# Sorting experts by load ahead of a branch, and three smaller moves in the order of work

## The chip, the cores and the metric

One core of a Trainium2 chip runs the whole kernel. The metric is the device time in microseconds. The engines are PE (TensorE: products; its weight loads have a row of their own, PEld), DVE (VectorE), ACT (ScalarE), POOL (GpSimd) and SP (SyncE, which here only issues DMAs and handles registers). A "q" behind an engine's name is its sequencer, which waits, branches and issues.

## The reference

Two decoder layers over 512 tokens of width 1024, each a mixer and then a mixture of 16 experts, with a last RMSNorm. What the change touches is the experts' part:

```python
def hier_moe(xn, w_group, b_group, w_router, b_router, w_gate, w_up, w_down):
    glog = tf @ w_group + b_group                       # 4 groups
    gval, gsel = lax.top_k(jax.nn.softmax(glog), 1)
    elog = jnp.einsum('td,dge->tge', tf, w_router) + b_router
    ...                                                 # the chosen group's 4 experts
    top_v, top_i = lax.top_k(elog_sel, TOP_K)           # 2 of 4
    top_w = jax.nn.softmax(top_v, axis=-1) * gval
    ...
    for g in range(N_GROUPS):
        h = silu(einsum('td,edf->tef', t, w_gate[g])) * einsum('td,edf->tef', t, w_up[g])
        out = out + einsum('tef,efd->td', h * combine[:, g, :, None], w_down[g])
```

Each token goes to two experts. An expert's weights are 1024x512 (gate), 1024x512 (up) and 512x1024 (down), 2 MB each in f32.

## The kernel before

**Order of the work.** The program is traced once, in the order of the Python code; a planner then orders each engine's instructions as a list: what is traced first goes first among what its estimated times hold ready, and an idle engine takes a later instruction that is ready. `tc.issue_after(x)` puts the instructions of its block behind `x` on `x`'s engine. A `tc.If` is planned as one piece. All loads of weights are issued by SP in one queue, in order; the router's rows go to DRAM from ACT's queue; gathers and scatters of token rows go from POOL's queue.

**Router** (`router`, `chosen_of`, `ranks`). The last product of the mixer yields the tokens in four chunks of 128. For each chunk the logits come from PE (L959 for the last chunk); VectorE scales the normed rows (`rows` in the changed code, L987, two halves), which are stored to `xnd` for later gathers, and computes the logits `lg` (L989) and from them, by comparisons, which experts each token takes (L897 to L907). PE sums masks, so that each token gets its place in the list of its expert (`pos`, L904).

**Experts' start** (`moe`). `loads` reduces the counts to one number `cmax` (L1039 to L1043). `gather(0)` brings expert 0's tokens together: two chunks by a gather from DRAM (L929, L1249), two by products with one-hot matrices (L1254, which read the rows and one-hots of chunks 2 and 3). Then every engine reads `cmax` (L1410) and branches (L1411): if any list is over 128, or more than the planned number of experts are over 64, a general path computes everything (`moe_any`); the inputs here do not take it, so each engine jumps over its code. Behind the branch `by_load` ranks the experts 2 to 15 by their count (five VectorE operations, L1054 to L1058), so that heavy ones take the steps `H` (128 rows, weights split into a high and a low half for three products each) and light ones the steps `L` (64 rows, plain f32) of

`STEPS = "HHHLHHLHLHHLHHLL"`

Experts 0 and 1 keep steps 0 and 1. A product turns the ranking into ids (L1060, copied by L1062), a second one sorts the columns of `pos` (L1064, L1065). SP reads the ids into registers (L1420) and from then on loads weights by id (L1190). `listed(e)` builds an expert's one-hot from `pos` (L1012 heavy, L1017 light), sums the token numbers on PE (L1024, L1025) and writes the index (L1027); `fetch(e)` gathers the rows (L1222).

**Splits** (`wsplit`, L194). Each quarter of a heavy weight takes one ACT operation (high half), one VectorE operation (low half; for two quarters at the start, POOL) and six PE products (L197 to L199). The halves live in a ring of three, later four tiles. Raw weights live in 14 tiles of 1 MB. In `proj`, expert 0's splits are held behind the router's last one-hot, and in `gather(0)` the split of the gathered tokens behind `cmax`. In `load` the down weights of expert 1 are held behind the reads of the ids.

**Router parameters** (`router_params`, L855 to L860). Five small loads on SP into single tiles; those of layer 1 are traced in the middle of layer 1's attention (`layer1_mix`), and the planner issues them as soon as layer 0's router has read its own.

Of the kernel before, what the change touches and what calls it, by code (L numbers as in the profile page):

```python
# [37 lines left out]
    0, 128, 256, 384, 388, 389, 405, 425, 426, 427  # L38

STEPS = "HHHLHHLHLHHLHHLL"  # L40
NS = NE - 2
NHEAVY = STEPS[2:].count("H")
LIGHT = 64
# [3 lines left out]
def _constants():  # L47
# [11 lines left out]
    e_ = p % 16  # L59
    e2 = np.arange(2, 16)  # L60
    th = np.where(e2[None, :] < e_[:, None], -0.5, 0.5)
    heavy, light = iter(range(NHEAVY)), iter(range(NHEAVY, NS))
    rank = [next(heavy) if k == "H" else next(light) for k in STEPS[2:]]
    blk = np.full((128, 4, NS), -1.0)
    for i in range(64):
        if i % 16 >= 2:
            blk[i, i // 16] = rank
    own = (np.arange(16)[None, :] == e_[:, None]).astype(np.float32)
    srt = np.concatenate([blk.reshape(128, 56), own, th], 1).astype(np.float32)
    cst[:, C_EC] = e_  # L70
# [25 lines left out]
def kernel(ctx: ExitStack, tc: tile.TileContext, I, out, *_):  # L96
# [686 lines left out]
    def layer1_mix(xT, first):  # L783
# [6 lines left out]
        for hf in range(2):  # L790
# [80 lines left out]
    def router(l, wr, br, wrb):  # L871
# [9 lines left out]
        if l == 0:  # L881
            srts.append(sm.tile([128, 208], F32, bufs=1, name="srt"))
            nc.scalar.dma_start(srts[0][:, 0:86], I["srt"])
        q.srt = srts[0]
# [87 lines left out]
        def chosen_of(c, pl, s0, s1):  # L972
            xn = F[9][:, 1024 * (c % 2):1024 * (c % 2) + 1024]
            if c < 3:
                s4 = m2([128, 128], "s4")
                S.copy(s4, pl)
                pl = bank(shape=(128, 20))
                PE.matmul(pl, s4, C[:, C_SEL:C_SEL + 20], start=True, stop=True)
            rs = rstd(s0, s1, q)
            if c > 1:  # L980
                q.xn.append(xn)
            for i in range(2):
                sl = slice(512 * i, 512 * i + 512)

                a, b, o = h[:, c, sl], grow[:, sl], xn[:, sl].rearrange("q (k p) -> q p k", k=4)
                a, b = (t.rearrange("q (p k) -> q p k", k=4) for t in (a, b))
                scaled.append(V.scalar_tensor_tensor(o, a, rs, b, op0=OP.mult, op1=OP.mult))  # L987
                nc.scalar.dma_start(xnd[c * 128:(c + 1) * 128, sl], xn[:, sl])
            V.scalar_tensor_tensor(lg[:, c, :], pl, rs, br, op0=OP.mult, op1=OP.add)  # L989
            ranks(c)  # L990

        return chunk, q

    def route(q):
# [40 lines left out]
        def loads():  # L1035

            cf = sm.tile([128, 1], F32, bufs=1, name="cf")
            more, m14 = srt[:, 118:119], srt[:, 102:102 + NS]
            V.tensor_reduce(cf, pp[:, 4, :], AX.X, OP.max)  # L1039
            V.tensor_scalar(m14, pp[:, 4, 2:NE], LIGHT + 0.5, CAP / NHEAVY, op0=OP.is_gt, op1=OP.mult)  # L1040
            V.tensor_reduce(more, m14, AX.X, OP.add)
            V.tensor_tensor(cf, cf, more, op=OP.max)
            loads.last = V.tensor_copy(cmax, cf)  # L1043
            pt = bank(shape=(64, 128))
            tr(pt, pos.rearrange("p c e -> p (c e)"))
            bT = m4s[1][0:64, 0:128]
            S.copy(bT, pt)
            return cf, bT

        def by_load(bT):  # L1050

            cnt, rank, own, gt = srt[0:64, 116:117], srt[0:64, 117:118], srt[0:64, 86:102], srt[0:64, 120:134]
            P = srt[0:64, 134:190]
            V.tensor_tensor(own, srt[0:64, 56:72], pp[0:64, 4, :], op=OP.mult)  # L1054
            V.tensor_reduce(cnt, own, AX.X, OP.add)
            V.scalar_tensor_tensor(gt, pp[0:64, 4, 2:NE], cnt, srt[0:64, 72:86], op0=OP.subtract, op1=OP.is_gt)
# [8 lines left out]
            V.tensor_copy(pos[:, :, 2:NE], pm)  # L1065
            return P, ids

        def weights(P=None, fits=None):
# [29 lines left out]
            if P is not None:  # L1098
                pt = bank(shape=(64, 128))
                tr(pt, wt.rearrange("p c e -> p (c e)"))  # L1100
                wT = m4s[1][0:64, 128:256]
                S.copy(wT, pt)
                pm = bank(shape=(128, NCH, NS))
                PE.matmul(pm.rearrange("p c s -> p (c s)"), wT, P, start=True, stop=True)
                V.tensor_copy(wt[:, :, 2:NE], pm)
                V.tensor_scalar(wt, wt, fits, None, op0=OP.mult)
# [66 lines left out]
    def moe(l, rt, norm, done, then=None):  # L1173
# [6 lines left out]
        def rows_of(e, w, r0, r1):  # L1180

            rows = "(k p)" if w == "w_down" else "(p k)"
            if e < 2:
# [42 lines left out]
        def gather(e):  # L1226
# [39 lines left out]
        def proj(e, w):  # L1266
# [153 lines left out]
        got, vals = nc.values_load_multi_w_load_instructions(  # L1420
            row[0:1, :], engines=(mybir.EngineType.SP,), min_val=0, max_val=NE - 1,
            skip_runtime_bounds_check_because="sums of one-hot rows: each is one of 2 to 15, or 0")
        ids.update(zip(range(2, NE), vals))
        ids[0] = got[-1]
        listed(2, range(2))
# [88 lines left out]
```

## Time and profile before

| | us |
|---|---|
| median of 3 runs (lowest, highest) | 1144.22 (1142.65, 1145.25) |
| profiled execution | 1145.4 |
| its span, first to last instruction | 1143.6 |
| PE busy | 1050.0 (92%) |
| VectorE busy | 734.0 (64%) |
| ScalarE busy | 562.2 (49%) |

The experts of layer 0 run from about 276 to 580 us of the span, those of layer 1 from about 824 to the end. Times of rows are counted from the span's start. An idle time in square brackets or behind a bar is that of the engine just before the row's instruction, with what released it as the semaphores suggest.

### The profile page before, as it was taken

What the parts mean: (1) busy time and instruction counts of PE and PEld (TensorE: products, weight loads), DVE (VectorE), ACT (ScalarE), POOL (GpSimd) and SP (SyncE); (2) the same over time, 40 slices, a digit from 0 to 9 for tenths busy, and PEclk for the clock granted to TensorE, in tenths of its full rate; (3) what the DMA queues carried; (4) which work ended last, traced back from release to release, by engine and by line L of the source; (5) the groups of instructions that cost most, each with busy time, mean ns of one, the idle gap of its engine ahead of it and who ended that gap; (6) DMA issues with size and microseconds to landing.
All of it is one profiled execution on the core that took longest, in us unless ns stands there. A gap on an engine that the chain in (4) does not pass through costs nothing. (4 is left out here: it accounts for less than half of the span.)

```text
span 1143.6 us, 15992 instructions
## 1 busy us (share of the span) xinstructions
PE 1050.0 (92%) x5951; PEld 762.0 (67%) x5951; DVE 734.0 (64%) x1265; ACT 562.2 (49%) x852; POOL 190.1 (17%) x120
## 2 busy tenths in 40 slices
PE   5979899998799999989889999999978999999994
PEld 4766677786576765757368777877756676565641
DVE  6988952777797755756372273275679785565634
ACT  5433134524576644655353353354366675464634
POOL 3734110000312221221000000000012132211111
PEclk9999999999999999999989999999999999989998
DMA  7262323356699999999842315226349999999963
GB/s 239 74 147 104 101 78 111 107 216 240 240 381 380 380 380 383 373 374 374 309 179 75 110 37 184 74 75 234 141 170 396 354 382 392 388 385 377 367 243 147
DMA packets 84712, 277.38 MB, mean 243 GB/s; under 512 B 23714, under 2 KB 23898, under 8 KB 68368
## 3 DMA queue, kind: packets, MB, share of 16 engines
q1 hardware_dynamic: 72000, 248.31, 57.7%
q0 software_dynamic: 8016, 16.88, 5.9%
q10 hardware_dynamic: 4608, 11.06, 2.6%
q8 instruction: 51, 0.84, 0.3%
q14 instruction: 37, 0.30, 0.1%
HBM read 262.49 MB, written 24.12 MB: 251 GB/s over the span
## 5 line engine op out<-in xcount | busy, mean ns | idle before, releaser
L198 PE MATMUL acc<-R,R 128*128 128x512 f32 x936 | 381.1, 407 | 17.1 <-DVE R L194 16.3
L197 PE MATMUL acc<-R,R 128*128 128x512 f32 x860 | 350.9, 409 | 26.3 <-ACT R L194 16.5
L199 PE MATMUL acc<-R,R 128*128 128x512 f32 x860 | 342.8, 401 | 1.3 <-DVE R L194 1.3
L194 DVE TENSOR_TENSOR R<-F,R 128x1024 fp32r<-128x1024 f32 (+1 forms) x178 | 212.9, 1218 | 138.1 <-ACT R L194 133.1
L194 ACT CAST R<-F 128x1024 fp32r<-128x1024 f32 (+1 forms) x178 | 182.4, 1040 | 180.6 <-PE acc L199 107.7
L198 PEld LDWEIGHTS acc<-R,R 128*128 128x128 f32 x936 | 179.2, 191 | 67.7 <-DVE R L194 28.9
L197 PEld LDWEIGHTS acc<-R,R 128*128 128x128 f32 x860 | 164.2, 191 | 67.7 <-ACT R L194 22.5
L199 PEld LDWEIGHTS acc<-R,R 128*128 128x128 f32 x860 | 164.8, 192 | 37.7 <-DVE R L194 3.3
L1222 POOL DMA_INDIRECT F<-xnd,idx x30 | 50.9, 1698 | 238.7 <-DVE ws L1032 113.9
L1304 PE MATMUL acc<-F,R 128*64 128x512 f32 x304 | 71.2, 595 | 0.0
L194 DVE TENSOR_TENSOR R<-pb,R 128x512 fp32r<-128x512 f32 x84 | 57.3, 702 | 14.6 <-ACT R L194 14.5
L1376 POOL DMA_INDIRECT hd<-m,idx x20 | 36.6, 1829 | 147.8 <-ACT m L1375 146.0
L194 ACT CAST R<-pb 128x512 fp32r<-128x512 f32 x84 | 47.5, 586 | 27.4 <-PE pb L190 20.9
L194 DVE TENSOR_TENSOR R<-R,R 128x1024 fp32r<-128x1024 f32 x40 | 48.2, 1221 | 6.4 <-ACT R L194 6.0
L922 POOL MEMSET R<- 128x1024 f32 x2 | 1.9, 954 | 300.6 <-PE acc L199 300.6
L1304 PEld LDWEIGHTS acc<-F,R 128*64 128x64 f32 x304 | 22.0, 137 | 43.6 <-issue 43.2
L194 ACT CAST R<-R 128x1024 fp32r<-128x1024 f32 x40 | 41.4, 1050 | 13.2 <-PE acc L199 12.1
L197 PE MATMUL acc<-spare,R 128*128 128x512 f32 x116 | 45.7, 394 | 0.0
L199 PE MATMUL acc<-spare,R 128*128 128x512 f32 x116 | 45.7, 394 | 0.0
L190 PE MATMUL pb<-C,F 128*128 128x128 f32 (+1 forms) x296 | 37.5, 261 | 3.4 <-POOL F L490 3.4
L190 PE MATMUL pb<-C,m 128*128 128x128 f32 (+1 forms) x163 | 27.7, 292 | 12.7 <-DVE m L227 9.6
L1307 ACT ACTIVATE m2w<-acc 64x512 f32<-64x512 f32 x8 | 4.7, 593 | 68.5 <-PE acc L1304 68.5
(384 smaller groups left out, 1447.0 us busy)
## 6 DMA issues: line engine op xcount, KB each, us to landing
F<-in_moe_w_up_dram SPq DMA_DIRECT2D x46, 1024.0 KB, 22.4
F<-in_moe_w_down_dram SPq DMA_DIRECT2D x40, 1024.0 KB, 22.2
F<-in_moe_w_gate_dram SPq DMA_DIRECT2D x38, 1024.0 KB, 23.0
R<-in_moe_w_gate_dram SPq DMA_DIRECT2D x20, 1024.0 KB, 15.9
R<-in_moe_w_down_dram SPq DMA_DIRECT2D x12, 1024.0 KB, 24.9
h<-in_moe_w_down_dram SPq DMA_DIRECT2D x12, 1024.0 KB, 22.5
F<-in_c_w_qkv_dram SPq DMA_DIRECT2D x12, 1024.0 KB, 6.1
F<-in_ab_w_in_dram SPq DMA_DIRECT2D x10, 1024.0 KB, 5.1
```

The lines of the kernel that those rows point to most:

```text
L190: PE.transpose(dst, src, ident[:n, :n])
L194: return S.copy(hi, src), eng.tensor_tensor(lo, src, hi.bitcast(F32), op=OP.subtract)
L197: PE.matmul(ps, ah, bh, start=first, stop=False)
L198: PE.matmul(ps, ah, bl, start=False, stop=False)
L199: return PE.matmul(ps, al, bh, start=False, stop=last)
L922: G.memset(q.x0, 0.0)
L1222: rows[e] = G.indirect_dma_start(out=xg[e % 2][0:n], out_offset=None, in_=xnd[:, :], in_offset=bass.IndirectOffsetOnAxis(ap=idx[0:n, e, 0: ...
L1304: m = PE.matmul(ps[LIGHT * i:LIGHT * i + LIGHT], x_[:, 4 * kk + k, :], raw[i][:, k, :], start=kk + k == 0, stop=kk + k == 4, skip_group_ch ...
L1307: silu = S.activation(hs[0:LIGHT], ps[LIGHT:2 * LIGHT], AF.Silu)
L1376: G.indirect_dma_start(out=hd[:, :], out_offset=bass.IndirectOffsetOnAxis(ap=idx[:, e, 1:2], axis=0), in_=y[:, :], in_offset=None, bounds_ ...
```

## The change

`by_load` is traced ahead of `gather(0)` and of the branch. The split of expert 0's gathered tokens and the splits of its gate weights are held behind the last rank operation. The down weights of expert 1 are no longer held behind the ids. For the last chunk the router's ranks are traced ahead of its rows. The parameters of layer 1's router are issued behind the last weight load traced before them. The constant 2 gets a name, with the columns of the table that depend on it.

```diff
@@ constants
+FIXED = 2
 STEPS = "HHHLHHLHLHHLHHLL"
-NS = NE - 2
-NHEAVY = STEPS[2:].count("H")
+NS = NE - FIXED
+NHEAVY = STEPS[FIXED:].count("H")
...
@@ layer1_mix
             if hf == 0:
-                params = router_params(1, nc.sync)
+                with tc.issue_after(fr.load.ins):
+                    params = router_params(1, nc.sync)
@@ router, chosen_of(c, pl, s0, s1)
-            for i in range(2):
-                ...
-                scaled.append(V.scalar_tensor_tensor(o, a, rs, b, op0=OP.mult, op1=OP.mult))
-                nc.scalar.dma_start(xnd[c * 128:(c + 1) * 128, sl], xn[:, sl])
+            def rows():
+                for i in range(2):
+                    ...
+                    scaled.append(V.scalar_tensor_tensor(o, a, rs, b, op0=OP.mult, op1=OP.mult))
+                    nc.scalar.dma_start(xnd[c * 128:(c + 1) * 128, sl], xn[:, sl])
+
+            if c < 3:
+                rows()
             V.scalar_tensor_tensor(lg[:, c, :], pl, rs, br, op0=OP.mult, op1=OP.add)
             ranks(c)
+            if c == 3:
+                rows()
@@ route, by_load(bT)
-            V.tensor_scalar(P, srt[0:64, 0:56], rank, None, op0=OP.is_equal)
+            by_load.last = V.tensor_scalar(P, srt[0:64, 0:4 * NS], rank, None, op0=OP.is_equal)
@@ moe, load(e, w, r0, r1)
-            with tc.issue_after(ids[0].ins) if (e, w) == (1, "w_down") else nullcontext():
-                fr.load = nc.sync.dma_start(t, rows_of(e, w, r0, r1))
+            fr.load = nc.sync.dma_start(t, rows_of(e, w, r0, r1))
@@ moe, gather(e)
-                with after(loads.last.ins) if e == 0 else nullcontext():
+                with after(by_load.last.ins) if e == 0 else nullcontext():
                     gather.last = split_to(xh[:, 4 * i:4 * i + 4], xl[:, 4 * i:4 * i + 4], pt)
@@ moe, proj(e, w)
-                    for i in (rt.last, rt.sqrt) + (gather.last if k2 else ()) if held else ():
+                    for i in (rt.last, rt.sqrt, by_load.last) + (gather.last if k2 else ()) if held else ():
@@ moe
         cf, bT = loads()
+        perm, row = by_load(bT)
         gather(0)
         top = nc.values_load(cmax[0:1, 0:1], min_val=0, max_val=T)
         with tc.If(top > CAP):
             moe_any(l, weights(), xg[1])
         table(AF.Silu)
         ...
-        perm, row = by_load(bT)
         listed(1, range(2))
         fetch(1)
         listed(0, range(2), rt.oh)
-        got, vals = nc.values_load_multi_w_load_instructions(
+        _, vals = nc.values_load_multi_w_load_instructions(
             row[0:1, :], engines=(mybir.EngineType.SP,), min_val=0, max_val=NE - 1,
             ...
-        ids[0] = got[-1]
```

## Rows read from the trace of the kernel before

**Rows 1.** The page's second part: busy tenths of PE and of DMA in 40 slices.

```profile
PE   5979899998799999989889999999978999999994
...
DMA  7262323356699999999842315226349999999963
```

**Rows 2.** Busy us of each engine, granted clock, DMA share, GB/s by stretch.

```profile
290.00:320.00 30.00, 24.35 (x134) 18.02 (x133) 25.02 (x43) 18.84 (x24) 9.36 (x5) 0.98 0.79 293
...
350.00:560.00 210.00, 200.91 (x996) 130.98 (x994) 132.53 (x169) 116.28 (x143) 39.65 (x22) 0.99 1.00 375
590.00:690.00 100.00, 100.00 (x478) 78.94 (x476) 43.94 (x86) 39.97 (x79) 0.00 (x0) 1.00 0.25 80
```

**Rows 3.** Waits of ScalarE from 296 to 560: who for whom, us, times, longest.

```profile
ACT R L194 <- DMA F<-in_moe_w_up_dram: 0.9, 1, 0.9
```

**Rows 4.** Waits of PE from 284 to 320.

```profile
PE acc L198 <- DVE R L194: 4.9, 2, 2.6
...
PE acc L197 <- ACT R L194: 0.7, 1, 0.7
```

**Rows 5.** PE in order of time: start us, us, line, operation, idle before it.

```profile
275.21 1.91 PE L959 MATMUL pb<-wrb,m 128*128 128x20 f32 x16
...
281.45 2.05 PE L1254 MATMUL acc<-m2w,F 128*128 128x128 f32 x16
288.08 0.77 PE L197 MATMUL acc<-R,R 128*128 128x512 f32 x1 [4.58 <-DVE srt L1058]
...
292.58 0.20 PE L1060 MATMUL pb<-srt,C 64*1 64x14 f32 x2
292.71 0.42 PE L1064 MATMUL pb<-srt,m 64*128 64x56 f32 x2
...
299.89 0.50 PE L198 MATMUL acc<-R,R 128*128 128x512 f32 x1 [2.60 <-DVE R L194]
```

**Rows 6.** VectorE in order of time, the same stretch of layer 0.

```profile
276.42 2.08 DVE L987 SCALAR_TENSOR_TENSOR F<-h,rs,growt 128x512 f32<-128x512 f32 x2
278.34 0.22 DVE L989 SCALAR_TENSOR_TENSOR lg<-pb,rs,wrb 128x20 f32<-128x20 f32 x1
...
281.58 0.15 DVE L1054 TENSOR_TENSOR srt<-srt,pb 64x16 f32<-64x16 f32 x1
...
287.75 0.24 DVE L1058 TENSOR_SCALAR srt<-srt 64x56 f32<-64x56 f32 x1
...
292.81 0.16 DVE L1062 CAST srt<-pb 1x14 int32<-1x14 f32 x1 [4.28 <-PE pb L1060]
...
295.68 2.89 DVE L1017 TENSOR_TENSOR junk<-C,pos 128x512 bf16<-128x512 f32 x1
...
298.63 1.21 DVE L194 TENSOR_TENSOR R<-F,R 128x1024 fp32r<-128x1024 f32 x1
```

**Rows 7.** Sequencers at the branch (L1410, L1411): duration ns min/median/max, first and last start.

```profile
L1410 PEldq TENSOR_LOAD <-cmax x2: 312/402/491, 283.8 to 832.7; - x2
...
L1411 PEldq COMPARE_BRANCH  x2: 3328/3378/3427, 284.4 to 833.2; - x2
...
L1411 DVEq COMPARE_BRANCH  x2: 56/64/72, 285.7 to 834.4; - x2
```

**Rows 8.** SP at L1420: its wait from 281 to 330, and its reads of the ids.

```profile
SPq L1420 <- DVE el L1081: 8.0, 1, 8.0
...
L1420 SPq TENSOR_LOAD <-srt x2: 2885/2888/2891, 293.0 to 841.8; - x2
```

**Rows 9.** Layer 1: VectorE at L1062, and waits of PE from 833 to 870.

```profile
841.64 0.16 DVE L1062 CAST srt<-pb 1x14 int32<-1x14 f32 x1 [4.21 <-PE pb L1060]
...
PE acc L198 <- DVE R L194: 5.0, 2, 2.6
```

**Rows 10.** Gathers by POOL (L1222), from 297.5 to 300 and from 842 to 846.

```profile
DMA to landing us min/median/max: 9.8/9.8/9.8
...
DMA to landing us min/median/max: 4.7/4.7/4.7
```

More of the change, by code (lines that the diff above doesn't have):

```diff
@@ L38 @@
     0, 128, 256, 384, 388, 389, 405, 425, 426, 427
+FIXED = 2
 STEPS = "HHHLHHLHLHHLHHLL"
-NS = NE - 2
-NHEAVY = STEPS[2:].count("H")
+NS = NE - FIXED
+NHEAVY = STEPS[FIXED:].count("H")
+S_OWN, S_TH, S_TAB = 4 * NS, 4 * NS + 16, 5 * NS + 16
 LIGHT = 64
@@ L59, in _constants @@
     e_ = p % 16
-    e2 = np.arange(2, 16)
+    e2 = np.arange(FIXED, NE)
     th = np.where(e2[None, :] < e_[:, None], -0.5, 0.5)
     heavy, light = iter(range(NHEAVY)), iter(range(NHEAVY, NS))
-    rank = [next(heavy) if k == "H" else next(light) for k in STEPS[2:]]
+    rank = [next(heavy) if k == "H" else next(light) for k in STEPS[FIXED:]]
     blk = np.full((128, 4, NS), -1.0)
     for i in range(64):
-        if i % 16 >= 2:
+        if i % 16 >= FIXED:
             blk[i, i // 16] = rank
     own = (np.arange(16)[None, :] == e_[:, None]).astype(np.float32)
-    srt = np.concatenate([blk.reshape(128, 56), own, th], 1).astype(np.float32)
+    srt = np.concatenate([blk.reshape(128, 4 * NS), own, th], 1).astype(np.float32)
     cst[:, C_EC] = e_
@@ L882, in router @@
             srts.append(sm.tile([128, 208], F32, bufs=1, name="srt"))
-            nc.scalar.dma_start(srts[0][:, 0:86], I["srt"])
+            nc.scalar.dma_start(srts[0][:, 0:S_TAB], I["srt"])
         q.srt = srts[0]
@@ L981, in chosen_of @@
                 q.xn.append(xn)
-            for i in range(2):
-                sl = slice(512 * i, 512 * i + 512)
-                a, b, o = h[:, c, sl], grow[:, sl], xn[:, sl].rearrange("q (k p) -> q p k", k=4)
-                a, b = (t.rearrange("q (p k) -> q p k", k=4) for t in (a, b))
-                scaled.append(V.scalar_tensor_tensor(o, a, rs, b, op0=OP.mult, op1=OP.mult))
-                nc.scalar.dma_start(xnd[c * 128:(c + 1) * 128, sl], xn[:, sl])
+            def rows():
+                for i in range(2):
+                    sl = slice(512 * i, 512 * i + 512)
+                    a, b, o = h[:, c, sl], grow[:, sl], xn[:, sl].rearrange("q (k p) -> q p k", k=4)
+                    a, b = (t.rearrange("q (p k) -> q p k", k=4) for t in (a, b))
+                    scaled.append(V.scalar_tensor_tensor(o, a, rs, b, op0=OP.mult, op1=OP.mult))
+                    nc.scalar.dma_start(xnd[c * 128:(c + 1) * 128, sl], xn[:, sl])
+            if c < 3:
+                rows()
             V.scalar_tensor_tensor(lg[:, c, :], pl, rs, br, op0=OP.mult, op1=OP.add)
             ranks(c)
+            if c == 3:
+                rows()
         return chunk, q
@@ L1039, in loads @@
             V.tensor_reduce(cf, pp[:, 4, :], AX.X, OP.max)
-            V.tensor_scalar(m14, pp[:, 4, 2:NE], LIGHT + 0.5, CAP / NHEAVY, op0=OP.is_gt, op1=OP.mult)
+            V.tensor_scalar(m14, pp[:, 4, FIXED:NE], LIGHT + 0.5, CAP / NHEAVY, op0=OP.is_gt, op1=OP.mult)
             V.tensor_reduce(more, m14, AX.X, OP.add)
@@ L1050, in by_load @@
         def by_load(bT):
-            cnt, rank, own, gt = srt[0:64, 116:117], srt[0:64, 117:118], srt[0:64, 86:102], srt[0:64, 120:134]
-            P = srt[0:64, 134:190]
-            V.tensor_tensor(own, srt[0:64, 56:72], pp[0:64, 4, :], op=OP.mult)
+            cnt, rank, own, gt = srt[0:64, 116:117], srt[0:64, 117:118], srt[0:64, 86:102], srt[0:64, 120:120 + NS]
+            P = srt[0:64, 134:134 + 4 * NS]
+            V.tensor_tensor(own, srt[0:64, S_OWN:S_TH], pp[0:64, 4, :], op=OP.mult)
             V.tensor_reduce(cnt, own, AX.X, OP.add)
-            V.scalar_tensor_tensor(gt, pp[0:64, 4, 2:NE], cnt, srt[0:64, 72:86], op0=OP.subtract, op1=OP.is_gt)
+            V.scalar_tensor_tensor(gt, pp[0:64, 4, FIXED:NE], cnt, srt[0:64, S_TH:S_TAB], op0=OP.subtract, op1=OP.is_gt)
             V.tensor_reduce(rank, gt, AX.X, OP.add)
-            V.tensor_scalar(P, srt[0:64, 0:56], rank, None, op0=OP.is_equal)
+            by_load.last = V.tensor_scalar(P, srt[0:64, 0:4 * NS], rank, None, op0=OP.is_equal)
             pi = bank(shape=(1, NS))
@@ L1064, in by_load @@
             PE.matmul(pm.rearrange("p c s -> p (c s)"), bT, P, start=True, stop=True)
-            V.tensor_copy(pos[:, :, 2:NE], pm)
+            V.tensor_copy(pos[:, :, FIXED:NE], pm)
             return P, ids
@@ L1104, in weights @@
                 PE.matmul(pm.rearrange("p c s -> p (c s)"), wT, P, start=True, stop=True)
-                V.tensor_copy(wt[:, :, 2:NE], pm)
+                V.tensor_copy(wt[:, :, FIXED:NE], pm)
                 V.tensor_scalar(wt, wt, fits, None, op0=OP.mult)
@@ L1182, in rows_of @@
             rows = "(k p)" if w == "w_down" else "(p k)"
-            if e < 2:
+            if e < FIXED:
                 return wv[w][e, r0:r1, :].rearrange(f"{rows} n -> p k n", p=128)
@@ L1419, in moe @@
         listed(0, range(2), rt.oh)
-        got, vals = nc.values_load_multi_w_load_instructions(
+        _, vals = nc.values_load_multi_w_load_instructions(
             row[0:1, :], engines=(mybir.EngineType.SP,), min_val=0, max_val=NE - 1,
-            skip_runtime_bounds_check_because="sums of one-hot rows: each is one of 2 to 15, or 0")
-        ids.update(zip(range(2, NE), vals))
-        ids[0] = got[-1]
+            skip_runtime_bounds_check_because="sums of one-hot rows: each is one of FIXED to 15, or 0")
+        ids.update(zip(range(FIXED, NE), vals))
         listed(2, range(2))
```

## The prediction

> **What bounds the kernel now.** I read the slices of the page first, then the busy time by stage, then who waits for whom, and last the two engines' instructions around the branch. In the slices PE is at 9 nearly throughout, and DMA is at 9 through both expert stages [rows 1]: two resources look full there. The windows tell more. In the middle of layer 0's experts (350 to 560) PE is busy 200.91 of 210 us and DMA has a share of 1.00; in layer 1's attention (590 to 690) PE is busy 100.00 of 100 us with DMA at 0.25 [rows 2]. So outside the start of the expert stage nothing but PE's own work sets the time, as long as weights arrive. They do: in all of layer 0's expert stage ScalarE, which takes each heavy weight tile first, has only two short waits for a transfer, the longer 0.9 us [rows 3]. What is left is the start of the stage: from 290 to 320 PE is busy only 24.35 of 30 us [rows 2]. Between 284 and 320 it waits 4.9 us in two pieces for VectorE's low halves (2.6 and 2.3 us) and 0.7 us for ScalarE [rows 4], and ahead of that it stands still for 4.58 us at the branch [rows 5]. The list puts those 4.58 us down to VectorE's L1058, but the row of the branch itself says otherwise: PE's read of the count takes 0.49 us from 283.8, its COMPARE_BRANCH 3.33 to 3.43 us from 284.4, while VectorE's takes 0.07 us [rows 7]. So PE's pause is its branch, and it resumes at 288.08.
>
> Why the two later waits? VectorE finishes the fifth operation of the ranking (L1058) at 287.99, does a few small ones, and then stands 4.28 us in front of L1062, the copy of the sorted ids, because L1060, the product that makes them, sits on PE behind the branch and twelve expert products, at 292.58 [rows 5, 6]. Everything behind L1062 in VectorE's order is then late: L1017 (one-hot of expert 3) runs from 295.68 for 2.89 us, and the low half that PE needs comes only at 298.63; PE starts again at 299.89 [rows 5, 6]. Layer 1 repeats it: 4.21 us idle in front of L1062 and PE waits of 5.0 us in two [rows 9].
>
> **The change, part by part, per layer.**
>
> *Sorting ahead of the branch.* No operation is added: the same five rank operations, two products and two copies run. By the trace the ranking was already partly ahead of VectorE's branch at 285.7; what really crosses is the end of it, L1060, L1064 and the copies. (a) PE: the two products take 292.58 to 293.06, 0.48 us [rows 5]. Put behind the gather's last product (ends 283.50) they end at 283.98; PE's read of the count starts at 283.8 today [rows 7], because the count is late, so 0.3 us are hidden and about 0.2 us push the branch: +0.2. If the count comes no earlier than now and the products are held by a late rank, it is more (the slower rival). (b) Behind the branch PE has 0.48 us less: -0.48. (c) VectorE has no reason to stand in front of L1062. Into the 4.28 us go the one-hot of expert 2, the index writes, L1017, and the first operations of the weights. PE's wait of 2.6 us stems from L1017 in front of a low half; with it done early the half follows its high half directly. Bounds: 0 (L1017 stays where it is) to -2.6; I take -2.6, since 4.28 us of room hold 2.89 us of work. (d) The second pair of waits, 2.3 and 0.7 us, lies further on, where VectorE is busy 25.02 of 30 us [rows 2] and catches up only slowly. Bounds 0 to -3.0; I take a third, -1.0, because its other work there stays.
>
> *The holds.* The gather's low half and expert 0's first split now wait for the last rank operation instead of for the count and the router. Queued behind them on VectorE are the other splits of expert 0; waiting for them is PE at 288.08. VectorE needs two operations of some 1.2 us each before PE's first product (L194 in rows 6 shows one). The ranking starts at 281.58 and its last operation takes 0.24 us [rows 6]; ten such operations, the count's five among them, end by 284 as an estimate, and 2.4 us of splits by 286.4, ahead of 288.08: 0. The cover is PE's branch; were it gone, each us of ranking would cost one.
>
> *Ranks ahead of rows, last chunk.* The two row operations take 2.08 us from 276.42, and the logits came behind them at 278.34 [rows 6]. The logits need PE's products, which end at 277.12 [rows 5], so they gain about 1 us. PE is packed from 275.21 to 283.50 with the router's and the gather's products, so this shortens nothing on PE: 0. The rows must be there when the gather's last products start at 281.45 [rows 5]; if they fill VectorE's wait for the rank's sums they end some 280 to 281: 0. Their two stores on ScalarE's queue shift with them; ScalarE needs to be free for the transposed positions only after that: 0.
>
> *SP: ids earlier, expert 1's down weights earlier.* SP waits 8.0 us at L1420 and then reads the ids for 2.89 us [rows 8]. Its first load by id goes out up to 8 us earlier, and the two 1 MB loads of expert 1, no longer behind the ids, can go as soon as their tiles are free, before the branch. This moves the stream ahead and gives PE nothing, since PE does not wait for weights [rows 3]: 0; it is the cover for (c) and (d), which make PE ask earlier. One thing runs against it: POOL's gather for expert 1 meets an emptier DMA today, and one landed in 4.7 us without the stream and in 9.8 with it [rows 10]. Bounds 0 to the 5.1 us between them; I take 0, since its index is written in VectorE's gap too, some us earlier.
>
> *Router parameters of layer 1 later.* Five small loads on SP's queue move from layer 0's router into the attention, behind a weight load. There PE is 100.00 of 100 us busy and DMA is at 0.25 [rows 2]; their issue can only delay a weight load by a few us where PE never stood still: 0. The renamed constants change nothing at FIXED = 2.
>
> **Sum.** +0.2 - 0.48 - 2.6 - 1.0 = -3.9 us per layer, -7.8 for two. The bounds of (c) and (d) give -0.3 to -5.9 per layer. The profiled execution took 1145.4 us (span 1143.6 and 1.8 around it), so 1137.6 by its own time; the median of the runs is 1.2 lower, 1144.22, which gives 1136.4.
>
> **Rivals.**
>
> *The gap isn't used.* The planner that orders each engine keeps the one-hot products behind the first expert products, and L1017 in front of the same low half. Then only (a) and (b) remain, up to -0.8 per layer: 1142.6 to 1143.6. For it: the order is a list order by estimated times, and a one-hot was left unmoved in today's gap. Against: what stood in front of it there was L1062, and that is gone.
>
> *Late rows (the slower side).* The rows of the last chunk are now written behind the ranks. If VectorE takes them only after the last rank operation of the chunk (about 281.4), they end at 283.5 instead of 278.5. The gather's last products then start at 283.5 instead of 281.45, +2.05, the branch follows, and the ranking with its held splits falls as much later on VectorE, so that these splits fill the 4.28 us instead of L1017 and (c) is lost too. Net +2.05 - 0.48, about +1.6 per layer: 1147.4. It decides from the point where the rows end after 281.45, and outweighs the gain above some 283. For it: the rows have become the lower of the two in the program's order. Against: VectorE must wait for PE's sums in the middle of the ranks, and the rows are ready then.
>
> *The stream is the bound.* DMA's share of 1.00 [rows 2] suggests that the end follows the stream. Then the 8.0 us of ids [rows 8] and the 2 MB at 375 GB/s [rows 2], 5.6 us, would be gained in each layer: 27.2 us, 1117.0. Against it stand ScalarE's waits [rows 3].
>
> *A slower branch.* PE's COMPARE_BRANCH takes 3.33 to 3.43 us where VectorE's takes 0.07 [rows 7], in a stretch with DMA all but idle. If what it waits for is a transfer, the earlier weight stream can slow it as it slows a gather, 9.8 us against 4.7 us [rows 10], by 2.1 times: +3.7 per layer, which leaves 1143.8 with the gain above. It needs the 2 MB still moving at 284.4, and issued before 276 they would be done by 282. The Trainium skill, "Runtime: NRT & Kernel Launch", section "Instruction fetch mechanics", has this rule: a taken branch to a target outside the fetched window forces a DMA fetch before the engine goes on. The long row on PE alone fits it; no row yet shows such a branch under traffic.
>
> **How the numbers follow.** Chances: forecast 0.56, gap unused 0.16, late rows 0.13, stream 0.07, slower branch 0.08. What the measurement can tell from no change is 0.2%, 2.3 us: faster means below 1141.9, slower above 1146.5. The forecast and the stream lie below, with a few hundredths of the others: 0.67 faster. The unused gap and the slower branch mostly lie within: 0.20. Late rows and a little more: 0.13 slower. The forecast's own range is 1132.4 (all of (c) and (d)) to 1140.5; the range of 8 in 10 goes from 1131.5 to 1145.0, which takes in the unused gap and leaves out the stream and the late rows.
>
> **What would show it.** Right: PE's COMPARE_BRANCH still 3.3 us and PE's restart within half a microsecond of now; L1062's counterpart ahead of the branch with no 4 us gap on VectorE behind it; PE's first wait of 2.6 us gone, the second shortened; SP's first load by id 5 to 8 us earlier, with no gain from it alone; both layers alike. Wrong: the gather's last products held by the rows, a branch above 4 us, PE waiting for the gather of expert 1, or the 2.6 us at their old place.

## The result, and the profile after

The changed kernel takes 1126.85 us, the kernel before 1143.45 us on the same chip: a ratio of 0.985, with an interval of 0.983 to 0.987. It is faster by 16.6 us, more than twice the 7.8 us that I forecast and outside my range. On a second chip (e8 below) the ratio was 0.984, with 0.981 to 0.986. To read single profiles: in each profiled execution the granted clock of TensorE is 1.2 instead of 2.4 GHz in seven to fourteen stretches, 37.5 to 73.8 us in all, in part at places that differ from one execution to the next. PE's busy time changes with it: the 497 products of the late experts in the tables below are busy for 99.86 us at a mean clock of 1.00, for 102.97 at 0.98 and for 105.81 at 0.95. So I compare PE's idle time stretch by stretch (length less PE busy), and let the timed rounds speak for the sum.

The table of stretches of the kernel before, then of the changed kernel: in each the first line is the start of layer 0's experts (from the gather's last products to expert 3), the second its late experts (from expert 8 to expert 14), the third and fourth the same of layer 1. Columns: stretch, length, busy us of PE, PE's weight loads, VectorE, ScalarE, POOL, granted clock, DMA share, GB/s.

```profile
278.83:348.82 69.99, 59.12 (x339) 45.67 (x337) 61.27 (x110) 46.95 (x57) 17.20 (x10) 0.98 0.78 287
428.72:539.15 110.43, 102.97 (x497) 68.67 (x496) 71.78 (x88) 64.19 (x78) 19.81 (x12) 0.98 1.01 377
827.74:899.00 71.26, 60.43 (x339) 46.66 (x337) 60.32 (x103) 46.98 (x57) 17.19 (x10) 0.95 0.73 280
978.45:1091.77 113.32, 105.81 (x497) 70.83 (x496) 71.82 (x88) 64.23 (x78) 19.63 (x12) 0.95 1.01 381
```

```profile
276.39:344.33 67.94, 59.96 (x339) 46.77 (x337) 61.70 (x110) 47.04 (x57) 16.25 (x10) 0.95 0.76 290
424.54:526.84 102.30, 99.86 (x497) 67.80 (x497) 69.43 (x87) 62.56 (x76) 19.85 (x11) 1.00 1.01 375
818.99:886.16 67.17, 58.77 (x339) 45.88 (x337) 60.37 (x105) 47.10 (x57) 16.79 (x10) 0.97 0.75 289
966.06:1068.07 102.01, 99.55 (x497) 67.82 (x496) 69.89 (x87) 62.47 (x76) 19.78 (x11) 1.00 1.01 375
```

Length less PE busy gives the idle time. At the start it falls from 10.9 and 10.8 us to 8.0 and 8.4: 5.3 us in both layers together, the part I had forecast (with 7.8). In the late experts it falls from 7.5 and 7.5 to 2.4 and 2.5: 10.1 us, of which my forecast has nothing. The rest, from expert 14 to the next stage or the end of the kernel, idles 3.7 us more than before (12.2 to 15.9 by the gaps between PE's instructions). Together that is 11.7 of the 16.6 us. The mean granted clock of the timed runs is 0.978, that of the kernel before 0.974 to 0.975 in the experiments below; 0.3 to 0.4% of 1143 us is some 4 us as an estimate, and where this part comes from stays open. DMA's share is 1.01 in the late experts of both kernels.

The start, as it answers to [rows 4] and [rows 5]: waits of PE from 280 to 316, then its instructions there in order of time (idle time before one in brackets).

```profile
PE pb L1035 <- PEq L1422: 3.6, 1, 3.6
PE pb L1115 <- ACT m L1113: 0.9, 1, 0.9
PE pb L1036 <- issue: 0.8, 1, 0.8
PE acc L201 <- ACT R L198: 0.7, 1, 0.7
PE acc L203 <- DVE R L198: 0.7, 1, 0.7
PE acc L202 <- DVE R L198: 0.5, 1, 0.5
```

```profile
281.05 0.20 PE L1071 MATMUL pb<-srt,C 64*1 64x14 f32 x2
281.18 0.43 PE L1075 MATMUL pb<-srt,m 64*128 64x56 f32 x2
285.19 0.16 PE L1035 MATMUL pb<-tl,junk 128*128 128x2 bf16 x1 [3.59 <-PEq L1422]
...
288.46 0.16 PE L1036 MATMUL pb<-rc,m2w 128*128 128x2 bf16 x1 [0.81 <-issue]
...
296.02 0.50 PE L202 MATMUL acc<-R,R 128*128 128x512 f32 x1 [0.54 <-DVE R L198]
```

The sort's two products stand ahead of the branch; the branch holds PE for 3.59 us instead of 4.58 [rows 5]; the wait of 2.60 us is 0.54, with a new one of 0.81 ahead of it, for which the profile names no engine (the last section has what stands beside it); the second pair, 2.32 and 0.73 us in the kernel before, is 0.70 and 0.73 with 0.89 on the way. PE's branch instruction, and SP's loads of expert 1's down weights and its first load by id (columns as in [rows 7]; for SP: start us, us, operation):

```profile
L1422 PEldq COMPARE_BRANCH  x2: 3368/3488/3607, 281.7 to 824.1; - x2
```

```profile
265.51 6.09 SPq L1200 DMA_DIRECT2D R<-in_moe_w_down_dram  x2
287.47 0.37 SPq L1200 DMA_DIRECT2D F<-in_moe_w_gate_dram  x1
```

The ids' first load goes at 287.47, where the kernel before waited 8.0 us for the ids and read them from 293.0 on [rows 8], and the down weights of expert 1 go at 265.51. The queues are full then, and these loads keep them at a share of 0.89 until 276, where the kernel before has 0.38 (the same stretch of both, the kernel before first; columns as in the first table):

```profile
270.00:276.00 6.00, 5.09 (x40) 4.10 (x32) 4.82 (x16) 2.71 (x8) 2.09 (x2) 1.00 0.38 113
270.00:276.00 6.00, 5.09 (x41) 4.53 (x41) 3.86 (x17) 2.37 (x5) 0.29 (x1) 1.00 0.89 290
```

The late experts hold the surprise. In the kernel before, PE's waits there name ScalarE (5.2 us) and VectorE (1.8 us), and ScalarE's longest waits name PE; no wait of the two names a transfer. Waits of PE, then of ScalarE, from 430 to 525, and ScalarE in order of time at the first of these places:

```profile
PE acc L197 <- ACT R L194: 5.2, 6, 1.6
PE acc L198 <- DVE R L194: 1.8, 3, 0.8
```

```profile
ACT m2w L1307 <- PE acc L1304: 22.4, 2, 12.1
ACT m L1382 <- PE acc L1326: 6.2, 2, 3.1
```

```profile
435.88 0.59 ACT L1307 ACTIVATE m2w<-acc 64x512 f32<-64x512 f32 x1 [12.10 <-PE acc L1304]
436.50 0.58 ACT L194 CAST R<-pb 128x512 fp32r<-128x512 f32 x1
436.98 1.05 ACT L194 CAST R<-F 128x1024 fp32r<-128x1024 f32 x1
```

ScalarE stands 12.10 us in front of a light expert's silu (L1307), which needs PE's products, while the heavy expert's down weights stand behind it in its list; PE then waits for their split. The weights were late as well: the second of the two loads that bring them is issued at 410.4 and takes 26.0 us, so it lands at 436.4, behind the start of the silu.

```profile
DMA to landing us min/median/max: 26.0/26.0/26.0
```

In the changed kernel the same place has the other order: the splits first, waiting for their transfer, the silu behind them. Columns as above.

```profile
425.03 1.04 ACT L198 CAST R<-F 128x1024 fp32r<-128x1024 f32 x1 [1.65 <-DMA F<-in_moe_w_down_dram]
425.98 1.04 ACT L198 CAST spare<-F 128x1024 fp32r<-128x1024 f32 x1
431.70 0.59 ACT L1317 ACTIVATE m2w<-acc 64x512 f32<-64x512 f32 x1 [4.68 <-PE acc L1314]
```

```profile
ACT R L198 <- DMA F<-in_moe_w_down_dram: 12.2, 4, 7.6
```

### The profile page after: what moved, and what is told of

It reads as the page before. It is cut to its first block, busy times and chain, and to the rows that moved or that the text cites. A ratio compares the mean times of both kernels' runs of the same rounds, so it can differ in the third digit from the quotient of the medians.

```text
span 1123.5 us, 16007 instructions
## 1 busy us (share of the span) xinstructions
PE 1044.2 (93%) x5951; PEld 761.6 (68%) x5951; DVE 730.7 (65%) x1265; ACT 564.2 (50%) x852; POOL 191.1 (17%) x120
## 5 line engine op out<-in xcount | busy, mean ns | idle before, releaser
L194 PEld LDWEIGHTS pb<-C,m 128*128 128x128 f32 (+1 forms) x163 | 20.4, 152 | 27.0 <-DVE m L231 10.3
```

The lines of the kernel that those rows point to most:

```text
L194: PE.transpose(dst, src, ident[:n, :n])
```

## Experiments

All ratios are to the kernel before, timed on the same chip in turn. START is my forecast (only the start of the stage counts), STREAM or LANDING says that weights which land earlier are the gain, ORDER that it is the engines' lists, which the planner writes anew for every edit.

**One part at a time, and the order of ScalarE.** e1 lists the light expert's scatter scale behind the next heavy expert's splits; e2 puts the changed kernel's splits behind that scale; e3 and e4 are the two large parts of the change alone.

```
e1, before:  with after(wsplit.hi.ins):
                 S.activation(y, ps, AF.Copy, scale=...)       # L1382
e2, changed: late() ahead of proj(e, "w_up") where a heavy expert follows a light one;
             for e = 9, 12 its first split stands in  with after(light_scatter.last.ins)
e3, before:  load() without  tc.issue_after(ids[0].ins)  for (1, "w_down")
e4, before:  by_load(bT) ahead of gather(0) and the branch, with the holds on by_load.last
```

> The kernel before, with one edit: the scale of a light expert's scatter (L1382) is listed on ScalarE behind the four high parts of the next expert's up weights, where that expert is heavy, two places per layer. PE's list and SP's list are unchanged. Theory ORDER (the gain of the late experts is the order of ScalarE's list): the two waits of 1.55 and 0.76 us at 458, 513, 1008 and 1065 us go, 9.2 us, and the low clock behind them, 6.8 us, less what the end of the stage gives back because the last light expert's weights land only 3.2 us ahead of their use: 1130 to 1138. Theory STREAM (the gain is weights that land earlier): the loads by id are issued as late as before, no gain, 1142 to 1145. Theory START (only the start of the expert stage counts, as I forecast): 1142 to 1145.

> The changed kernel, with the first high part of the up weights of experts 9 and 12 listed on ScalarE behind the light expert's scatter scale, as the kernel before has it. SP's list is that of the changed kernel. ORDER: gives back 5 to 14 us, 1132 to 1140, with PE's two waits back at those two places of each layer. STREAM: the weights land as early as in the changed kernel, 1125 to 1128. START: 1125 to 1128.

> The kernel before, with the one edit that expert 1's down weights are no longer held behind the ids. START: nothing waits for these weights, 1142 to 1145. STREAM: most of the gain, 1127 to 1132. ORDER: its ScalarE list has the scatter scale of expert 8 behind the four high parts, but that of expert 11 ahead of them as before; so the waits at 458 and 1008 go with their low clock (2.3+1.7 and 2.3+3.4) and those at 513 and 1065 stay: 1133 to 1138.

> The kernel before, with the sort and its holds ahead of the branch; expert 1's down weights stay behind the ids, the rows stay ahead of the ranks, the router parameters early. START: the start of the expert stage alone, 2.0 us in layer 0 and 4.1 in layer 1 by the shift of PE's work in the changed kernel, so 1136 to 1138. STREAM: the ids come 8 us earlier in each layer, 1127 to 1131. ORDER: the start's 6 us, and of the late waits those behind expert 8 in part (its scale stands behind two of the four high parts): 1130 to 1135.

Measured: e1 0.996 (0.994 to 0.998), e2 0.986 (0.983 to 0.989), e3 0.994 (0.992 to 0.996), e4 0.988 (0.985 to 0.990). START falls with e3: these loads cost nothing by my reckoning, and freeing them alone gives 7 us. STREAM as I had put it falls too: e3 has half of what it asked for. ORDER does not do well by e1: the waits at 458 us and its like don't go, they change their name.

```profile
PE acc L198 <- DVE R L194: 3.9, 4, 1.7
PE acc L197 <- ACT R L194: 2.2, 4, 0.6
```

VectorE's list holds the low parts now as ScalarE's had held the high ones. e2 brings back waits of 1.55 and 0.76 us at all four places, though SP's list is that of the changed kernel, so those waits are the list's; but its late idle time is 4.8 us per layer, the changed kernel's own waits (0.55 and 1.24 us) having gone, and in time it loses 1 to 2 us by the ratios, where ORDER asked for 5 to 14; its four runs spread so far (1127.75 to 1136.04 us) that 5 is not ruled out. The late idle time of e3 (4.6 and 5.2 us) and e4 (3.9 and 4.8) lies half way between the two kernels: each alone loses the first group of waits in a layer (438 and 458 us in the kernel before) and keeps the second. In both a short wait of PE names a transfer of gate weights now (0.7 and 1.3 us in e3, 0.9 in one layer of e4). Their gains add up to 21 us, the change has 17.

**Orders fixed by hand, the small edits, a repeat.**

```
e5 = e1 and, where a heavy expert follows a light one:
        pu = proj(e, "w_up")
        with after(wsplit.hi.ins):
            gather(e + 1)
e6 = the same in the changed kernel
e7 = before with  if c == 3: rows()  behind ranks(c), and
     with tc.issue_after(fr.load.ins): params = router_params(1, nc.sync)
```

> The kernel before, with the order fixed by hand at the places where a heavy expert follows a light one (up of experts 4, 7, 9 and 12): its up projection is traced ahead of the next gather, and the gather's rows and the light expert's scatter scale are listed on ScalarE behind the four high parts. SP's list, and so the weight stream, is that of the kernel before. ORDER: the waits of 1.55 and 0.76 us at 458, 513, 1008 and 1065 us go on both engines' lists now, 9.2 us, with a part of the low clock behind them (0 to 6.8 us), less up to 2 us per layer at the end of the stage: 1131 to 1138. STREAM: no load is issued earlier for it, 1142 to 1146. START: 1142 to 1146.

> The changed kernel with the same hand-fixed order. ORDER: its own late waits are 0.55 and 1.24 us per layer (490, 502, 1031, 1043 us), 3.6 us at most to win, but its last light expert's weights land with 0.0 us to spare, so most of it comes back as waits for transfers: 1124 to 1128, not told from the changed kernel. If it wins all of 3.6 us the end of the stage isn't bound by the stream. STREAM: no change, 1125 to 1128.

> The kernel before with the two small edits alone: the router's last ranks ahead of its rows, and the router parameters of layer 1 behind a weight load. The lists of PE, ScalarE and POOL are those of the kernel before. All theories: no change, 0 within 2 us; if one of them gains more than 2 us, it is a part of the gain that I gave to the sort and to the down weights.

> The changed kernel once more, on the chip of the three runs above: 17 us below the kernel before, as in its first runs. PE's idle time in the late experts again 2.4 us per layer where the kernel before has 7.5. Where the low clock stands differs from execution to execution and tells nothing of the change: if its windows lie elsewhere than in the first profile and the time is the same, it is no part of the gain.

Measured: e5 0.997 (0.995 to 0.998), e6 0.983 (0.980 to 0.985), e7 1.003 (1.001 to 1.006), e8 0.984 (0.981 to 0.986). e5 misses what ORDER asked: the late idle time is 6.3 us, VectorE's list still stands in front. e6 is the changed kernel again. e7 gains nothing and misses its "within 2 us" on the slow side: PE's and ScalarE's lists and the late idle time (7.5 us per layer) are those of the kernel before. Its 0.3% go with a granted clock of 0.972 in the mean of its runs against 0.974; its twelve runs lie from 1143.67 to 1155.06 us, and why half of them are above 1151 stays open.

**Orders fixed on both engines, and a copy that computes nothing.** e9 and e10 hold VectorE's part as well and put the light silu behind the splits ahead of it. e11 and e12 give the changed kernel a copy from DRAM to DRAM; between these two, only its size differs and no list.

```
e9, e10 (before, changed):
         with after(wsplit.hi.ins), after(wsplit.lo.ins):
             gather(e + 1)                   # and, behind down(e), the light silu
e11:  with tc.issue_after(table(AF.Silu).ins):
          nc.scalar.dma_start(extra[l], w_up_of_expert_15[0:64 rows])    # 128 KB
e12:  the same with all of it                                            # 2 MB
```

> The kernel before, with the order of the late experts fixed by hand on both VectorE and ScalarE: where a heavy expert follows a light one, the next gather's rows, its index work and the light scatter scale stand behind all high and low parts of the up weights; and a light expert's silu stands behind the splits of the heavy down weights ahead of it. SP's list is that of the kernel before. In the kernel before and in the first hand-fixed order PE idles 7.5 and 6.3 us per layer in the late experts, in the changed kernel 2.4. ORDER (the weights had landed long enough before, only the lists held them): 2 to 4 us per layer, and no new waits for transfers; 4 to 9 us below the kernel before. LANDING (a list can only split what has landed, so the earlier stream was needed): waits for weights take the place of the old ones, under 1.5 us per layer gained; within 3 us of the first hand-fixed order.

> The changed kernel with the same second hand-fixed order. Its late experts idle 2.4 us per layer; if the order fixed by hand is better still, up to 1.8 us per layer go, and the end of the stage, where weights land 0.0 us ahead of their use, gives back as much: 1123 to 1129, not told from the changed kernel. If it is slower by more than 2 us, the planner's own order is better than mine.

> The changed kernel with one more transfer on ScalarE's queue at the start of each expert stage, 128 KB from DRAM to DRAM: it is the control of the next run, whose lists on all engines are the same. Within 4 us of the changed kernel, by whatever the lists differ.

> As the run before, with 2 MB copied instead of 128 KB: the lists of all engines are the same, only the weight stream is later, by 5.6 us per layer at the 375 GB/s of the middle of the stage if a copy costs what a load does, up to 11 us if its read and its write each do. STREAM at the end of the stage (weights land 0.0 us ahead of use for the last light experts): all of it is lost, 11 to 22 us slower than the control, and the lost time stands as waits for transfers in the last experts. ORDER (the waits of the late experts come from the lists, not from the landings): the two pairs of waits of the kernel before don't return; where PE waits it is named a transfer. If the stream had room, 0 to 4 us.

Measured: e9 0.994 (0.992 to 0.997), late idle time 5.3 us; e10 0.984 (0.982 to 0.986); e11 0.979 (0.977 to 0.980); e12 0.979 (0.977 to 0.981). e9 is between its two theories: it gains 2.2 us of late idle time per layer, as ORDER asked, but ScalarE waits 16.6 us for down weights there, as LANDING asked. e11 is the find: a transfer that nobody needs makes the changed kernel about 6 us faster, 1120.74 us where the kernel before takes 1146.31. It beats both kernels. The late experts of e11 (columns as in the first table):

```profile
427.35:527.12 99.77, 99.14 (x498) 67.98 (x497) 69.03 (x86) 61.48 (x75) 18.59 (x11) 1.00 1.02 380
965.95:1065.38 99.43, 98.78 (x498) 68.04 (x497) 69.12 (x86) 61.52 (x75) 19.39 (x11) 1.00 1.01 382
```

Only 0.6 and 0.7 us of idle time are left. In time e12 can't be told from it; my estimate of 11 to 22 us was wrong because the 2 MB go when the queues have room, as e13 and e14 show.

**The copy in the kernel before.** Nothing of the change is in it; ScalarE's list becomes that of e11 (but for the place of one small activation per layer), PE's and VectorE's lists are new as well, and the loads of weights stand where the kernel before has them.

> The kernel before, nothing of the change in it, with a transfer of 128 KB from DRAM to DRAM on ScalarE's queue at the start of each expert stage. The planner's list for ScalarE is then the one of the changed kernel with the same transfer; SP's list keeps the sort's ids and expert 1's down weights where the kernel before has them. ORDER: PE's idle time in the late experts falls from 7.5 to about 0.6 us per layer with nothing loaded earlier, the start of the stage stays as before; 7 us per layer less what the end of the stage gives back (weights of the last light expert had 3.2 us to spare): 1130 to 1137 where the kernel before takes 1144 to 1146. LANDING: the splits wait for their weights instead; late idle 5 us or more per layer, 1139 to 1146.

> As the run before, with 2 MB copied; all lists are the same, the stream later by up to 5.6 us per layer. ORDER with room: within 3 us of the run before. LANDING, or no room left: 5 to 11 us slower than the run before, with PE or ScalarE waiting for transfers in the late experts.

Measured: e13 0.991 (0.989 to 0.994), 1135.97 us; e14 0.992 (0.990 to 0.995), 1136.19 us. So 10 us (7 to 13 by the interval) come from lists that any edit may bring: of the idle time, 8.7 us go in the late experts, and 3.9 come back behind them. Late experts of e13, and ScalarE's waits for transfers there:

```profile
429.57:534.03 104.46, 100.81 (x498) 69.35 (x497) 71.43 (x88) 64.48 (x78) 19.82 (x12) 0.98 1.00 372
978.74:1082.06 103.32, 100.66 (x498) 69.19 (x497) 71.70 (x88) 64.47 (x78) 19.20 (x11) 0.98 1.00 375
```

```profile
ACT R L195 <- DMA F<-in_moe_w_down_dram: 21.1, 4, 9.8
```

The idle time is 3.7 and 2.7 us, and ScalarE, which in [rows 3] had one short wait for a transfer, now waits 21.1 us for down weights in four pieces. The stream was late all along, as the load that landed at 436.4 in the kernel before says too; the old list had put the splits behind PE's own products, so that no wait named it. Where the extra 2 MB of e14 go, e13 first:

```profile
284.00:288.00 4.00, 0.00 (x0) 0.00 (x0) 3.85 (x11) 3.24 (x4) 0.00 (x0) 0.66 0.04 10
288.00:292.00 4.00, 3.90 (x9) 3.14 (x10) 0.28 (x2) 0.97 (x1) 0.00 (x0) 0.50 0.15 39
...
300.00:310.00 10.00, 8.47 (x42) 7.01 (x43) 9.33 (x21) 6.17 (x8) 2.25 (x2) 0.83 1.01 402
```

```profile
284.00:288.00 4.00, 1.51 (x5) 1.26 (x6) 2.62 (x9) 1.73 (x3) 0.00 (x0) 0.88 0.75 254
288.00:292.00 4.00, 4.00 (x30) 2.95 (x29) 0.50 (x3) 2.33 (x2) 0.00 (x0) 0.70 0.70 279
...
300.00:310.00 10.00, 10.00 (x47) 8.24 (x47) 8.96 (x17) 7.35 (x9) 1.95 (x1) 0.80 1.01 404
```

From 284 to 292 the queues carry 254 and 279 GB/s instead of 10 and 39, while SP waits for the ids; from 300 on both kernels have a share of 1.01. What moves before that point is free, what stands behind it is in the full stream.

**The stream alone, with equal lists.** With the copy in, PE's, VectorE's and ScalarE's lists can be kept while SP's changes.

```
e15 = e13 and e3 (down weights not behind the ids):    against e13 only SP's list differs
e16 = e13 and e4 (sort ahead of the branch)
```

> The kernel before with the copy of 128 KB, and expert 1's down weights no longer behind the ids. Against the kernel before with the copy only SP's list differs: two loads of 1 MB per layer stand ahead of the ids. START (nothing waits for weights, as I forecast): the same as that kernel, 1134 to 1138. LANDING (with such lists the splits wait for the stream, 2 MB are 5.6 us): ScalarE's waits for transfers in layer 0's late experts, 21 us there, fall to a third or less, PE's late idle from 3.6 and 2.7 to 1 us or less, and the end of the stage loses its waits for transfers: 4 to 9 us faster than that kernel, 1127 to 1132.

> The kernel before with the copy and with the sort and its holds ahead of the branch; the down weights stay behind the ids. Against the changed kernel with the copy (1120.7 us) PE's and ScalarE's lists are the same, VectorE's differs by the ranks, SP's by the down weights. START: the start of the stage is all there is beside the lists, so the same as that kernel within 2 us, and 5 to 6 us faster than the kernel before with the copy would be 1129 to 1131 if the rest of that difference is the stream. LANDING: 3 to 8 us slower than the changed kernel with the copy, 1124 to 1129, with waits of ScalarE for transfers in the late experts between its 3 us and the 21 us of the kernel before with the copy.

Measured: e15 0.980 (0.977 to 0.982), 1123.23 us, below what either theory gave it; e16 0.980 (0.977 to 0.983), 1122.41 us, below LANDING's 1124 to 1129 and within the 2 us around e11 that START allowed. Late experts of e15 and ScalarE's waits for the down weights:

```profile
428.27:528.07 99.80, 99.18 (x498) 68.01 (x497) 69.13 (x86) 61.48 (x75) 18.78 (x11) 1.00 1.01 382
967.33:1066.82 99.49, 98.81 (x497) 68.00 (x496) 69.13 (x86) 61.55 (x75) 18.79 (x11) 1.00 1.01 381
```

```profile
ACT R L199 <- DMA F<-in_moe_w_down_dram: 4.1, 1, 4.1
```

21.1 us of waits for transfers become 4.1, the idle time 0.6 us, and the time falls by 13 us (0.991 to 0.980). PE's idle time over the whole execution (the sum of the gaps before its instructions) accounts for half of that, 70.2 to 64.1 us; the other half goes with the clock, whose mean over the runs is 0.971 in e13 and 0.976 in e15 (0.5% of 1130 us is 5.6 us, as an estimate). So two loads of 1 MB, 5.6 us of stream per layer at 375 GB/s [rows 2], are worth 6 us of idle time in both layers, half of their length, once the lists let the splits go first; that the clock's half follows from them too is not shown. e16 reaches the same time by the sort and its earlier ids, its start idling 14.8 us against 20.5 in e15, and both together (e11) have 0.979: the first of the two shifts brings the late weights in time, the second finds little left. That fits the parts of the change not adding up.

The kernels side by side; idle time of PE in the late experts of layers 0 and 1, and the mean granted clock of the timed runs (of the kernel before beside them 0.974 to 0.975):

| kernel | ratio | late idle, us | clock |
|---|---|---|---|
| before | 1 | 7.5, 7.5 | 0.974 |
| down weights free (e3) | 0.994 | 4.6, 5.2 | 0.977 |
| sort ahead (e4) | 0.988 | 3.9, 4.8 | 0.977 |
| changed (e8) | 0.984 | 2.4, 2.6 | 0.978 |
| before + copy (e13) | 0.991 | 3.7, 2.7 | 0.971 |
| before + copy, down weights free (e15) | 0.980 | 0.6, 0.7 | 0.976 |
| before + copy, sort ahead (e16) | 0.980 | 0.6, 0.7 | 0.975 |
| changed + copy (e11) | 0.979 | 0.6, 0.7 | 0.974 |

## Why the prediction was wrong

The step that failed is the one on SP: "This moves the stream ahead and gives PE nothing, since PE does not wait for weights [rows 3]: 0". [rows 3] is right as a row: ScalarE hardly waits for a transfer. The inference is wrong. In these lists, which each engine goes through in order, other work stands in front of a split (the silu that held ScalarE for 12.10 us); then the wait bears that work's name, and in the late experts it read PE for ScalarE and ScalarE for PE. That the planner puts other work there where its estimates have a weight late is how I read it; no trace shows the estimates. The runs show two terms in the place of my 0: the lists (e13: 10 us with no load listed earlier) and the landing (e15 against e13: 13 us, of which 6 are idle time and the rest goes with the clock, with PE's, VectorE's and ScalarE's lists equal). In the lists that the planner made without the copy, the same shift gives 7 us (e3).

The sign was already in what I quoted. [rows 2] has PE busy 200.91 of 210 us between 350 and 560, beside a DMA share of 1.00; I read that as "nothing but PE's own work". The missing 9.1 us per layer are more than the 4.9 and 0.7 us of [rows 4] on which I built the sum. My rival "the stream is the bound" had the right resource, a chance of 0.07 and a price of 27.2 us, taken as if every us of stream were one of time. In the change the late experts and the end of the stage gave 6.4 us of idle time, a quarter of that, because the late experts idle only 7.5 us per layer and the end of the stage gives some back.

The steps at the start of the stage were right in mechanism; they brought two thirds of the forecast, 5.3 us of idle time in both layers against 7.8.
- (a) and (b), the two products: I had +0.2 and -0.48; PE's pause at the branch fell by 1.0 us (4.58 to 3.59) in layer 0 and 0.8 in layer 1, because PE's read of the count (at 281.1 instead of 283.8) no longer comes behind its last product ahead of the branch.
- (c), the first wait: -2.6 forecast; 2.60 became 0.54, but 0.81 us stand new ahead of it, so -1.3 in layer 0. In layer 1 2.62 became 1.73, -0.9. VectorE has no gap of 4 us any more, as forecast.
- (d), the second pair: -1.0 forecast; 3.05 us became 2.32 with the new 0.89 counted, -0.7.
- The holds, the ranks ahead of the rows and the router parameters: 0 forecast. No idle time went with the last two (e7; VectorE writes the last rows by 277.1, the gather's last products start at 279.02). The holds were not run by themselves. The rivals "late rows" and "the gap isn't used" are out.
- The branch: 3.37 to 3.61 us against 3.33 to 3.43 [rows 7], so "a slower branch" is out here. What the branch waits for can be read, by its times, in the trace's transfers: in all 36 branches of the 18 profiles one packet of 16 KiB runs on the queue that the page calls instruction (q8), and the branch ends 1.27 to 1.37 us after that packet. The rule that I cited, the Trainium skill, "Runtime: NRT & Kernel Launch", section "Instruction fetch mechanics", agrees with these rows; which code the packet holds they don't show. The longest branch, 3.91 us in e12, is not the copy's doing: its packet was in at 284.3, ScalarE issues the copy at 284.4, and e5, which has no copy, has a branch of 3.89 us.

What stays open: which estimates lead the planner to its lists; and why e16, which idles 7 us less than e15 over its profiled execution (56.8 against 64.1 us), is not faster. Its profile has 67.1 us at the low clock, that of e15 51.6, and PE is busy 1052.0 against 1044.1 us with as many products, which is worth as much; whether that is chance or follows from the shorter waits, five runs each don't tell. Nor is it shown that the clock follows the waits: e13 has the lowest mean and e15, with fewer waits, 0.976, but e11, with as few in the late experts and fewer over the whole, has 0.974. And not all of e13's 10 us is accounted for: beside the 8.7 and 3.9 us in and behind the late experts its start idles 1.2 us less, and its mean clock is the lower one; ahead of the first experts the one profile of the kernel before idles 31.2 us, all other profiles 26.3 to 28.9, among them that of e7, whose PE and ScalarE have the same lists there.

## What to carry to other kernels

Where a planner writes the lists, "nobody waits for a transfer" doesn't mean that transfers are early enough: take the length of a full-DMA stretch less the busy time of its main engine, and if engines there name each other in a ring, look at what stands behind the waiting instruction. Test an edit against a null edit as well, such as a small copy at the same place: here the null edit alone moved the time by 10 us. A load that can go before the full stretch can save time (here 6 us of idle time for 11.2 us of stream), but only until the last weight lands ahead of its use.

## What the runs showed of the hardware

A copy of 2 MB from DRAM to DRAM, issued while the weight queue waited for ids, brought the queues to 254 to 279 GB/s in all and cost nothing that the timed runs tell apart (1136.19 against 1135.97 us, and 1122.26 against 1120.74). In the profile of e12 it costs something nearby all the same: PE is busy only 0.91 us between 288 and 292, and stands still for 5.86 us, with no engine named.

```profile
288.00:292.00 4.00, 0.91 (x9) 0.33 (x8) 0.32 (x1) 0.00 (x0) 0.07 (x1) 0.50 0.78 275
294.77 0.16 PE L1037 MATMUL pb<-rc,m2w 128*128 128x2 bf16 x1 [5.86 <-issue]
```

The trace has the reason at hand, though one case proves little. After the packet inside the branch, the instruction queue's next one begins 3.0 to 3.7 us later in the other 35 branches; here it begins 9.0 us later, at 292.36, when the copy's queue has moved its 2.10 MB (284.3 to 292.3), and PE goes on 1.4 us after that packet. The 0.81 us that the changed kernel has new ends in the same way, 1.5 us after such a packet. In the other three branches with 2 MB behind them (layer 1 of e12, both of e14) the packet isn't late. It is not made up for either: the start of layer 0 idles 13.0 us against 7.9 in e11, and the profiled execution is 3.2 us longer (1124.11 against 1120.96 us); the timed runs of e11 and e12 overlap.
